# Score products of attention in a two-layer hybrid block: one fp32 matmul per map, or a sum of three fp32r products of split queries and keys

## The chip, the cores and the metric

The kernel runs on one core of a Trainium2 chip. The metric is the device time of one launch in microseconds (us), as the median of several launches. A core has a matrix engine (TensorE, in the profile PE, with its weight loads listed apart as PEld), a vector engine (VectorE, DVE), a scalar engine for activations and copies (ScalarE, ACT), a general engine (GpSimd, POOL) and a sync engine (SyncE, SP) that issues most DMAs. Each engine runs its own list of instructions in order, and they meet at semaphores. Matrix products land in PSUM, everything else lies in SBUF, both with 128 partitions.

## The reference

Two layers, each a half-step SwiGLU, a token mixing, and another half-step SwiGLU. Every one of these is wrapped in RMS norms and modulated by shift, scale and gate that come from a conditioning vector ("adaLN"). There are 256 latent tokens and 128 prompt tokens, 1024 channels wide. The mixing has one input projection whose columns feed four groups; two of them are attentions. The change is in their scores:

```python
s = jnp.einsum("bqhmd,bshmd->bhmqs", qb, k).astype(jnp.float32) * scale   # differential
p = jax.nn.softmax(s, axis=-1)
w = p[:, :, 0] - lam * p[:, :, 1]
...
s = jnp.einsum("bqkgd,bskd->bkgqs", qb, k).astype(jnp.float32) * scale    # grouped-query
p = jax.nn.softmax(s, axis=-1)
```

Differential attention has 4 heads with 2 maps each and keys of 32 channels; grouped-query attention has 4 query heads on 2 key heads of 64 channels. Latent queries see 128 cached context keys and the 256 latent keys, so 384; prompt queries see the 128 prompt keys. All inputs and outputs are fp32.

## The kernel before, in words

The 384 tokens are three tiles of 128 rows, t = 0 and 1 latent, t = 2 prompt. The stages follow each other: FFN, mixing, FFN, in each of two layers. The big products are written as sums of three products in a faster matmul type, fp32r: each fp32 operand is split into an upper half (its value cast to fp32r) and a lower half (what the cast left out), and the product is upper x upper + upper x lower + lower x upper (`mm3_b`, L541 to L544; `mm3_a`, L546 to L550; `rows_out`, L576 to L578). Weights come from memory in 128x1024 tiles `st` (DMA on SP's queue, L156), are cast by ScalarE (L167) and subtracted by VectorE (L168) into a tile `wu` that holds both halves. Tiles `ast` (L269) carry the adaLN weights, of which VectorE makes weighted sums during the FFNs (L279).

In the mixing stage (`mix`, L695; about 312 to 480 us in the first layer and 1070 to 1238 us in the second) the projection is computed in pieces, and while TensorE works on a later piece, the rows of an earlier one are normed, rotated and turned: `d_tail` (L844) transposes queries and keys of the grouped-query attention into PSUM, and ScalarE copies them to `qTg` and `kTg`; `qk_tail` does the same for the differential attention into `qTd` and `kTd` (L1005, L1007, L1008). The cached keys come already transposed, by two DMAs on POOL's queue straight into the first 128 columns of `kTd` and `kTg`. A convolution with 31 taps runs beside all this as a long row of VectorE instructions on `cacc` (L799).

`probs` (L868) makes one attention map: one plain fp32 matmul into a PSUM bank (L871), the negative row maximum by VectorE (L872), the exponential with its row sum by ScalarE (L876). The contraction is over 32 partitions (differential, two maps of a head on neighbouring groups of 32) or 64 (grouped-query). Then come three transposes of the map (L886), a copy (L888), and the products with the values (L894). A unit for each head, in three parts, is threaded between the pieces of projection. The order that results on each engine is set by a scheduler in the framework, which moves instructions within their dependencies, so the row of instructions isn't quite that of the code.

## Time and profile before

| | us |
|---|---|
| median of 3 runs | 1563.77 |
| lowest and highest of them | 1561.25, 1564.76 |
| the profiled execution | 1562.17 |
| its span, first to last instruction | 1560.4 |

TensorE's granted clock over the span is 0.986 of full speed. The profile lists each engine's instructions with start and duration. A plain fp32 matmul leaves two records, an fp32r one leaves one. A matmul's recorded duration holds its fill and drain, so successive matmuls overlap in the records, and what one takes of the engine's time is the distance from its start to the next start. In the timeline, rows of one kind that follow each other are joined, with their count behind an x; what stands in brackets is the idle time ahead of an instruction and what ended it.

### The profile page before, as it was taken

Reading aid. Unit: us, or ns where it says so; the run is one execution under the profiler, and the core shown is the slowest. Engines: PE = TensorE matmul, PEld = TensorE weight load, DVE = VectorE, ACT = ScalarE, POOL = GpSimd, SP = SyncE. Lnnn points to the kernel's source line nnn. Section 1 sums busy time; section 2 is a strip of 40 time slices with the busy share of each in tenths; the row PEclk is TensorE's granted clock in tenths of the full one; section 3 lists DMA queues with packets and bytes.
Section 4 is the critical chain, followed back from the end, with each engine's and each line's share of the span. In section 5 each row is a group of like instructions: output and inputs, shape, how many; then the busy total and the mean of one; then the engine's idle time right before and its main releaser. Section 6 shows DMA issues by size and latency. Waiting matters only on the chain. (4 is left out here: it accounts for less than half of the span.)

```text
span 1560.4 us, 20661 instructions
## 1 busy us (share of the span) xinstructions
PE 1500.0 (96%) x7924; PEld 1319.9 (85%) x7924; DVE 1050.7 (67%) x1454; ACT 633.7 (41%) x1103; POOL 126.4 (8%) x234
## 2 busy tenths in 40 slices
PE   6899999999999999999999999999999999999997
PEld 3699998776887899998879999887768879999885
DVE  3678879867887845677586766984788796333432
ACT  3442233263466632334263333434545764323331
POOL 1101000021001201000021000002100120000000
PEclk9999999998999999999999999999999999999998
DMA  8668767733224555675546656773322245444431
GB/s 307 227 222 261 236 211 236 245 109 98 68 70 145 150 177 179 212 233 172 189 150 215 206 188 200 231 234 110 112 73 92 72 160 175 134 132 138 135 122 41
DMA packets 73619, 260.13 MB, mean 167 GB/s; under 512 B 9728, under 2 KB 9856, under 8 KB 73520
## 3 DMA queue, kind: packets, MB, share of 16 engines
q1 hardware_dynamic: 68112, 246.32, 48.5%
q0 software_dynamic: 4976, 11.70, 2.7%
q8 instruction: 62, 1.02, 0.3%
q10 hardware_dynamic: 432, 0.79, 0.1%
q14 instruction: 37, 0.30, 0.1%
HBM read 256.36 MB, written 2.41 MB: 166 GB/s over the span
## 5 line engine op out<-in xcount | busy, mean ns | idle before, releaser
L168 DVE TENSOR_TENSOR wu<-st,wu 128x1024 fp32r<-128x1024 f32 x322 | 391.6, 1219 | 296.5 <-ACT wu L167 295.9
L167 ACT CAST wu<-st 128x1024 fp32r<-128x1024 f32 x322 | 337.0, 1050 | 585.4 <-DMA st<-ws 253.7
L549 PE MATMUL ps_f<-h,wu 128*128 128x384 f32 x1248 | 418.6, 335 | 0.0
L548 PE MATMUL ps_f<-h,wu 128*128 128x384 f32 x1248 | 418.4, 336 | 0.0
L550 PE MATMUL ps_f<-h,wu 128*128 128x384 f32 x1248 | 418.3, 335 | 0.0
L279 DVE SCALAR_TENSOR_TENSOR acc<-ast,sc,acc 128x1024 f32<-128x1024 f32 x224 | 281.6, 1281 | 27.5 <-DMA ast<-w_ada 26.9
L548 PEld LDWEIGHTS ps_f<-h,wu 128*128 128x128 f32 x1248 | 234.9, 188 | 7.8 <-issue 4.2
L550 PEld LDWEIGHTS ps_f<-h,wu 128*128 128x128 f32 x1248 | 235.0, 188 | 0.0
L549 PEld LDWEIGHTS ps_f<-h,wu 128*128 128x128 f32 x1248 | 235.0, 188 | 0.0
L576 PE MATMUL ps_o<-wu,hid_s 128*128 128x512 f32 x528 | 206.5, 391 | 0.0
L577 PE MATMUL ps_o<-wu,hid_s 128*128 128x512 f32 x528 | 206.0, 390 | 0.0
L578 PE MATMUL ps_o<-wu,hid_s 128*128 128x512 f32 x528 | 205.5, 389 | 0.0
L576 PEld LDWEIGHTS ps_o<-wu,hid_s 128*128 128x128 f32 x528 | 99.1, 188 | 26.1 <-issue 5.9
L578 PEld LDWEIGHTS ps_o<-wu,hid_s 128*128 128x128 f32 x528 | 99.1, 188 | 20.6
L577 PEld LDWEIGHTS ps_o<-wu,hid_s 128*128 128x128 f32 x528 | 99.1, 188 | 20.0
L543 PE MATMUL ps_j<-wu,h 128*128 128x512 f32 (+1 forms) x192 | 73.1, 381 | 5.3 <-DVE wu L168 5.3
L542 PE MATMUL ps_j<-wu,h 128*128 128x512 f32 (+1 forms) x192 | 74.5, 388 | 0.0
L544 PE MATMUL ps_j<-wu,h 128*128 128x512 f32 (+1 forms) x192 | 72.6, 378 | 0.0
L676 ACT ACTIVATE sg<-ps_f 128x384 f32<-128x384 f32 x78 | 38.0, 487 | 83.4 <-PE ps_f L550 79.3
L799 DVE SCALAR_TENSOR_TENSOR cacc<-upad,late,cacc 128x399 f32<-128x399 f32 x120 | 69.9, 630 | 0.0
L337 POOL DMA_DIRECT2D gd<-grow x24 | 11.7, 496 | 676.0 <-DVE grow L329 676.0
L677 DVE TENSOR_TENSOR hid<-sg,ps_f 128x384 f32<-128x384 f32 x78 | 42.9, 549 | 23.3 <-PE ps_f L550 23.3
(234 smaller groups left out, 1701.0 us busy)
## 6 DMA issues: line engine op xcount, KB each, us to landing
st<-ws SPq DMA_DIRECT2D x320, 512.0 KB, 3.9
ast<-w_ada SPq DMA_DIRECT2D x128, 512.0 KB, 4.4
a<-ada SPq DMA_DIRECT2D x16, 512.0 KB, 9.3
G<-gd POOLq DMA_DIRECT2D x12, 512.0 KB, 4.7
brow<-b_ada POOLq DMA_DIRECT2D x24, 64.0 KB, 5.6
prow<-norm_post POOLq DMA_DIRECT2D x24, 64.0 KB, 6.1
x<-x_sample SPq DMA_DIRECT2D x2, 512.0 KB, 5.2
x<-x_prompt SPq DMA_DIRECT2D x1, 512.0 KB, 8.9
```

What stands on the lines that cost most here:

```text
L167: nc.scalar.copy(out=u[:, 0, :], in_=x)
L168: nc.vector.tensor_tensor(out=u[:, 1, :], in0=x, in1=u[:, 0, :].bitcast(F32), op=ALU.subtract)
L279: nc.vector.scalar_tensor_tensor(out=self.acc[c], in0=w, scalar=s1, in1=self.acc[c], op0=ALU.mult, op1=ALU.add)
L542: nc.tensor.matmul(out, lhsT=hk(h, k, 0, tsl), rhs=wh, start=start, stop=False)
L543: nc.tensor.matmul(out, lhsT=hk(h, k, 0, tsl), rhs=wl, start=False, stop=False)
L544: nc.tensor.matmul(out, lhsT=hk(h, k, 1, tsl), rhs=wh, start=False, stop=stop)
L548: nc.tensor.matmul(out, lhsT=wh, rhs=hk(h, k, 0, sl), start=start, stop=False)
L549: nc.tensor.matmul(out, lhsT=wh, rhs=hk(h, k, 1, sl), start=False, stop=False)
L550: nc.tensor.matmul(out, lhsT=wl, rhs=hk(h, k, 0, sl), start=False, stop=stop)
L576: nc.tensor.matmul(out, lhsT=pr[:, 0, s, tsl], rhs=u[:, 0, hsl], start=(q == 0), stop=False)
L577: nc.tensor.matmul(out, lhsT=pr[:, 0, s, tsl], rhs=u[:, 1, hsl], start=False, stop=False)
L578: nc.tensor.matmul(out, lhsT=pr[:, 1, s, tsl], rhs=u[:, 0, hsl], start=False, stop=(q == n - 1))
```

## The change

The score of a map becomes three fp32r products over split queries and keys, accumulated in the same PSUM bank: upper x upper, upper x lower, lower x upper. Queries and keys therefore hold both halves, in tiles with one more dimension of 2. A new helper `halves` makes them: the upper one is ScalarE's copy, as before but in type fp32r, the lower one is a new VectorE instruction that reads the same source and subtracts the upper half. The two maps of a differential head are now issued together, product by product in turn; the scheduler moves these too. The cached keys come by one DMA into a buffer `kc` and are split from there.

The larger tiles need room in SBUF. The pool of the `ast` tiles moves from the whole kernel into each FFN's scope; the scratch `sink` of the squares is half as wide; the wide copy of the conditioning vector goes to the setup's pool; `grow` has one buffer instead of two; the buffers of type `c3` are three instead of four, with one of their own for `upad` and `zT`.

```diff
-    ap_ = ctx.enter_context(tc.tile_pool(name="adap", bufs=2))
...
-        with tc.tile_pool(name=nm("fp"), bufs=1) as fp:
+        with tc.tile_pool(name=nm("fp"), bufs=1) as fp, tc.tile_pool(name=nm("adap"), bufs=2) as ap_:
...
-            kTd = mp.tile([P, 2, TOK], F32, name=nm("kTd"))
+            kTd = mp.tile([P, 2, 2, TOK], F32R, name=nm("kTd"))
...
-            nc.gpsimd.dma_start(out=kTd[:, :, 0:P], in_=a["cache_kT"][l, :, 0:2])
-            nc.gpsimd.dma_start(out=kTg[:, 0:P], in_=a["cache_kT"][l, :, 2])
+            kc = mp.tile([P, TOK], F32, tag="p", name=nm("kc"), bufs=4)
+            nc.gpsimd.dma_start(out=kc.rearrange("p (c n) -> p c n", c=3), in_=a["cache_kT"][l])
+
+            def halves(hi, lo, src, scale=1.0):
+                nc.scalar.mul(hi, src, scale)
+                nc.vector.scalar_tensor_tensor(
+                    out=lo, in0=src, scalar=scale, in1=hi.bitcast(F32), op0=ALU.mult, op1=ALU.subtract
+                )
...
+            halves(kTd[:, 0, :, 0:P], kTd[:, 1, :, 0:P], kc[:, 0:256].rearrange("p (c n) -> p c n", c=2))
+            halves(kTg[:, 0, 0:P], kTg[:, 1, 0:P], kc[:, 256:384])
...
-                nc.scalar.mul(
-                    qTg[:, :, t * P : (t + 1) * P], pt[:, 0:256].rearrange("p (g n) -> p g n", g=2), 64 ** -0.5
-                )
-                nc.scalar.copy(out=kTg[:, (t + 1) * P : (t + 2) * P] if t < 2 else kTgp, in_=pt[:, 256:384])
+                tsl, ksl = slice(t * P, (t + 1) * P), slice((t + 1) * P, (t + 2) * P)
+                halves(
+                    qTg[:, 0, :, tsl], qTg[:, 1, :, tsl], pt[:, 0:256].rearrange("p (g n) -> p g n", g=2),
+                    64 ** -0.5,
+                )
+                k0, k1 = (kTg[:, s, ksl] if t < 2 else kTgp[:, s, :] for s in range(2))
+                halves(k0, k1, pt[:, 256:384])
...
-            def probs(t, st, idx, lhsT, rhs):
+            def probs(t, st, maps):
+
                 nk = TOK if t < 2 else P
-                ps = bank(nm("ps_s"))
-                nc.tensor.matmul(ps[:, 0:nk], lhsT=lhsT, rhs=rhs, start=True, stop=True)
...
+                pss = [bank(nm("ps_s")) for _ in maps]
+                for a_, b_ in ((0, 0), (0, 1), (1, 0)):
+                    for ps, (idx, lhsT, rhs) in zip(pss, maps):
+                        nc.tensor.matmul(
+                            ps[:, 0:nk], lhsT=lhsT(a_), rhs=rhs(b_), start=(a_ + b_ == 0), stop=(a_ == 1)
+                        )
...
-                        r = 32 * (2 * (hd % 2) + m)
-                        pm.append(probs(t, st, i0 + m, qTd[r : r + 32, c, tsl], kt[r : r + 32, c, :]))
+                    rows = [slice(32 * (2 * (hd % 2) + m), 32 * (2 * (hd % 2) + m) + 32) for m in range(2)]
+                    pm = probs(
+                        t, st,
+                        [
+                            (i0 + m, lambda s, r=r: qTd[r, s, c, tsl], lambda s, r=r: kt[r, s, c, :])
+                            for m, r in enumerate(rows)
+                        ],
+                    )
...
-                nc.scalar.mul(qTd[:, :, t * P : (t + 1) * P], pq[:, 0:2, :], 32 ** -0.5)
-                nc.scalar.copy(out=kTd[:, :, (t + 1) * P : (t + 2) * P] if t < 2 else kTdp, in_=pq[:, 2:4, :])
+                tsl, ksl = slice(t * P, (t + 1) * P), slice((t + 1) * P, (t + 2) * P)
+                halves(qTd[:, 0, :, tsl], qTd[:, 1, :, tsl], pq[:, 0:2, :], 32 ** -0.5)
+                k0, k1 = (kTd[:, s, :, ksl] if t < 2 else kTdp[:, s] for s in range(2))
+                halves(k0, k1, pq[:, 2:4, :])
```

The order on the engines changes as follows. In its rows the names are those of the code with running numbers (`ps_j` a projection's PSUM bank, `ps_s` a map's, `wu` a split weight tile, `h` the normed input).

TensorE at the first two latent maps of the grouped-query attention in the first layer, before:

```order
L544 MATMUL ps_j325_3117<-wu76_2952,h235_2555 128x512
L871 MATMUL ps_s328_3137<-kTg282_2809,qTg284_2811 128x384
L542 MATMUL ps_j325_3117<-wu76_2952,h235_2555 128x512
L543 MATMUL ps_j325_3117<-wu76_2952,h235_2555 128x512
L544 MATMUL ps_j325_3117<-wu76_2952,h235_2555 128x512
L542 MATMUL ps_j325_3117<-wu77_3112,h236_2556 128x512
L543 MATMUL ps_j325_3117<-wu77_3112,h236_2556 128x512
L544 MATMUL ps_j325_3117<-wu77_3112,h236_2556 128x512
L542 MATMUL ps_j325_3117<-wu77_3112,h236_2556 128x512
L543 MATMUL ps_j325_3117<-wu77_3112,h236_2556 128x512
L544 MATMUL ps_j325_3117<-wu77_3112,h236_2556 128x512
L871 MATMUL ps_s332_3169<-kTg282_2809,qTg284_2811 128x384
```

and after the change:

```order
L545 MATMUL ps_j327_3126<-wu77_3121,h237_2558 128x512
L887 MATMUL ps_s330_3148<-kTg283_2812,qTg285_2814 128x384
L543 MATMUL ps_j327_3126<-wu77_3121,h237_2558 128x512
L544 MATMUL ps_j327_3126<-wu77_3121,h237_2558 128x512
L545 MATMUL ps_j327_3126<-wu77_3121,h237_2558 128x512
L887 MATMUL ps_s334_3182<-kTg283_2812,qTg285_2814 128x384
L887 MATMUL ps_s330_3148<-kTg283_2812,qTg285_2814 128x384 x2
L887 MATMUL ps_s334_3182<-kTg283_2812,qTg285_2814 128x384 x2
```

The two maps stood nine projection products apart. Now the first product of the first map stands alone, and its other two follow, with all three of the second map, after three projection products.

TensorE at the seventh pair of differential maps of the first layer (`ps_pT` are transposes of earlier maps, `ps_pv` products with values), before:

```order
L886 MATMUL ps_pT456_3841<-early_87,p435_3749 128x128 x3
L894 MATMUL ps_pv424_3700<-Vd285_2812,wt449_3804 128x64 x3
L871 MATMUL ps_s463_3862<-kTd279_2806,qTd281_2808 128x384
L871 MATMUL ps_s465_3867<-kTd279_2806,qTd281_2808 128x384
L548 MATMUL ps_j455_3828<-h235_2555,wu83_3495 128x384
```

and after:

```order
L551 MATMUL ps_j457_3895<-h235_2556,wu82_3482 128x384
L887 MATMUL ps_s465_3929<-kTd280_2809,qTd282_2811 128x384
L907 MATMUL ps_pT450_3863<-early_84,p429_3768 128x128 x3
L887 MATMUL ps_s466_3930<-kTd280_2809,qTd282_2811 128x384
L887 MATMUL ps_s465_3929<-kTd280_2809,qTd282_2811 128x384
L887 MATMUL ps_s466_3930<-kTd280_2809,qTd282_2811 128x384
L887 MATMUL ps_s465_3929<-kTd280_2809,qTd282_2811 128x384
L907 MATMUL ps_pT458_3908<-early_84,p438_3814 128x128 x3
L915 MATMUL ps_pv426_3755<-Vd286_2815,wt451_3867 128x64 x3
L887 MATMUL ps_s466_3930<-kTd280_2809,qTd282_2811 128x384
```

The pair's two matmuls stood side by side; its six products now stand in three places, with transposes between them, and in the middle one they alternate between the two banks.

VectorE ahead of the weight split that ends TensorE's wait at 378 us (rows 7 below), in the first layer (`dr` are rotated rows, `cacc` the convolution, `ss` is the sum of squares from which POOL makes the root `rstd`, `dn` the normed rows, `rt` a rotated part, `st` the row maxima), before:

```order
L726 TENSOR_TENSOR dr314_3049<-dn313_3044,late_89 128x384
L799 SCALAR_TENSOR_TENSOR cacc298_2936<-upad289_2820,late_89,cacc298_2936 128x399
L731 TENSOR_TENSOR dr314_3049<-dr314_3049,rt315_3050 128x384
L799 SCALAR_TENSOR_TENSOR cacc298_2936<-upad289_2820,late_89,cacc298_2936 128x399 x2
L814 TENSOR_REDUCE ss6319_3094<-sqd318_3090 128x6
L799 SCALAR_TENSOR_TENSOR cacc298_2936<-upad289_2820,late_89,cacc298_2936 128x399
L820 TENSOR_TENSOR dn322_3100<-ps_j316_3059,rstd321_3098 128x2x2x64
L826 TENSOR_TENSOR dn322_3100<-ps_j316_3059,rstd321_3098 128x128
L831 TENSOR_TENSOR dn322_3100<-dn322_3100,gqk_126 128x256
L831 TENSOR_TENSOR dn322_3100<-dn322_3100,gqk_126 128x128
L168 TENSOR_TENSOR wu77_3112<-st77_2950,wu77_3112 128x1024
L168 TENSOR_TENSOR wu78_3160<-st78_2955,wu78_3160 128x1024
```

and after:

```order
L733 TENSOR_TENSOR dr316_3056<-dn315_3051,late_86 128x384
L715 SCALAR_TENSOR_TENSOR qTg285_2814<-ps_dT319_3079,qTg285_2814 128x2x128
L738 TENSOR_TENSOR dr316_3056<-dr316_3056,rt317_3057 128x384
L715 SCALAR_TENSOR_TENSOR kTg283_2812<-ps_dT319_3079,kTg283_2812 128x128
L806 SCALAR_TENSOR_TENSOR cacc300_2939<-upad291_2823,late_86,cacc300_2939 128x399 x2
L824 TENSOR_REDUCE ss6321_3103<-sqd320_3099 128x6
L806 SCALAR_TENSOR_TENSOR cacc300_2939<-upad291_2823,late_86,cacc300_2939 128x399
L830 TENSOR_TENSOR dn324_3109<-ps_j318_3066,rstd323_3107 128x2x2x64
L836 TENSOR_TENSOR dn324_3109<-ps_j318_3066,rstd323_3107 128x128
L841 TENSOR_TENSOR dn324_3109<-dn324_3109,gqk_125 128x256
L841 TENSOR_TENSOR dn324_3109<-dn324_3109,gqk_125 128x128
L168 TENSOR_TENSOR wu77_3121<-st77_2957,wu77_3121 128x1024
```

Between the rotation of the tile before (`dr`) and the sum of squares, two lower halves (L715) now stand, and two convolution instructions (`cacc`) where there were three; the third stands further up, ahead of the first tile's sum of squares. The next rows are another lower half between the first weight split and the second, and one behind the second, ahead of the first row maximum.

## Rows read from the trace of the kernel before

**Rows 1.** From the page: busy time of each engine, its share of the span and its instructions; and the shares by engine of the chain of work that ended last.

```profile
PE 1500.0 (96%) x7924; PEld 1319.9 (85%) x7924; DVE 1050.7 (67%) x1454; ACT 633.7 (41%) x1103; POOL 126.4 (8%) x234
...
PE 41%; DVE 2%; POOL 1%; issue 1%; ACT 1%; DMA 1%; DVEq 0%; POOLq 0%; ACTq 0%
```

**Rows 2.** Busy time of the engines in the two mixing stages: the stretch and its length, busy us of PE, PEld, DVE, ACT and POOL (with instructions), TensorE's granted clock, DMA share, GB/s.

```profile
312.00:480.00 168.00, 159.35 (x826) 128.06 (x827) 126.74 (x270) 92.32 (x223) 22.92 (x43) 0.96 0.26 83
1070.00:1238.00 168.00, 159.63 (x843) 128.16 (x841) 127.54 (x274) 94.99 (x229) 23.35 (x43) 0.98 0.26 85
```

**Rows 3.** Groups of the score line on TensorE: tiles, shape, count of records, busy us in total and mean ns of one, idle time before.

```profile
L871 PE MATMUL ps_s<-kTd,qTd 32*128 32x384 f32 x64 | 19.4, 533 | 0.0
...
L871 PE MATMUL ps_s<-kTg,qTg 64*128 64x384 f32 x32 | 16.0, 583 | 0.0
...
L871 PE MATMUL ps_s<-kTdp,qTd 32*128 32x128 f32 x32 | 3.9, 321 | 0.0
...
L871 PE MATMUL ps_s<-kTgp,qTg 64*128 64x128 f32 x16 | 3.9, 322 | 0.0
```

**Rows 4.** TensorE's timeline at a lone latent map of the grouped-query attention, and at a lone prompt map: start, duration, line, operation.

```profile
373.09 0.39 PE L543 MATMUL ps_j<-wu,h 128*128 128x512 f32 x1
373.32 0.40 PE L544 MATMUL ps_j<-wu,h 128*128 128x512 f32 x1
373.65 0.91 PE L871 MATMUL ps_s<-kTg,qTg 64*128 64x384 f32 x2
374.49 0.50 PE L542 MATMUL ps_j<-wu,h 128*128 128x512 f32 x1
374.82 0.40 PE L543 MATMUL ps_j<-wu,h 128*128 128x512 f32 x1
...
412.31 0.48 PE L871 MATMUL ps_s<-kTgp,qTg 64*128 64x128 f32 x2
412.73 0.44 PE L903 MATMUL ps_mo<-early,mo 128*128 128x128 f32 x2
```

**Rows 5.** TensorE's timeline at three pairs of differential maps, two of latent and one of prompt queries, each with the instruction behind it.

```profile
435.88 0.91 PE L871 MATMUL ps_s<-kTd,qTd 32*128 32x384 f32 x4
436.73 0.45 PE L549 MATMUL ps_j<-h,wu 128*128 128x384 f32 x1
...
440.18 1.23 PE L871 MATMUL ps_s<-kTd,qTd 32*128 32x384 f32 x4
441.34 0.45 PE L548 MATMUL ps_j<-h,wu 128*128 128x384 f32 x1
...
463.93 0.49 PE L871 MATMUL ps_s<-kTdp,qTd 32*128 32x128 f32 x4
464.35 0.44 PE L548 MATMUL ps_j<-h,wu 128*128 128x384 f32 x1
```

**Rows 6.** TensorE's timeline in the projections: neighbouring fp32r products over all 128 rows, on 256 and on 384 columns.

```profile
408.64 0.29 PE L544 MATMUL ps_j<-wu,h 128*128 128x256 f32 x1
408.76 0.28 PE L542 MATMUL ps_j<-wu,h 128*128 128x256 f32 x1
...
433.13 0.34 PE L550 MATMUL ps_j<-h,wu 128*128 128x384 f32 x1
433.31 0.34 PE L548 MATMUL ps_j<-h,wu 128*128 128x384 f32 x1
```

**Rows 7.** The stall of the first layer's mixing: TensorE's instruction that ended it, VectorE's timeline ahead of it, and VectorE's busy time in three stretches behind it (stretch, length, busy us, TensorE's granted clock, DMA share, GB/s).

```profile
378.30 0.80 PE L543 MATMUL ps_j<-wu,h 128*128 128x512 f32 x1 [2.62 <-DVE wu L168]
...
375.96 0.42 DVE L820 TENSOR_TENSOR dn<-ps_j,rstd 128x256 f32<-128x256 f32 x1 [1.51 <-POOL rstd L460]
376.30 0.28 DVE L826 TENSOR_TENSOR dn<-ps_j,rstd 128x128 f32<-128x128 f32 x1
376.50 0.62 DVE L831 TENSOR_TENSOR dn<-dn,gqk 128x256 f32<-128x256 f32 x2
377.03 2.36 DVE L168 TENSOR_TENSOR wu<-st,wu 128x1024 fp32r<-128x1024 f32 x2
...
380.00:390.00 10.00, 8.21 (x16) 0.60 0.43 143
390.00:400.00 10.00, 8.99 (x18) 1.00 0.16 52
400.00:410.00 10.00, 9.15 (x18) 1.00 0.04 14
```

**Rows 8.** Groups of VectorE instructions with a PSUM source on 128x256 and 128x128.

```profile
L465 DVE TENSOR_TENSOR mTd<-ps_mo,mTd 128x256 fp32r<-128x256 f32 x6 | 2.5, 413 | 1.9 <-ACT mTd L464 1.9
...
L826 DVE TENSOR_TENSOR dn<-ps_j,rstd 128x128 f32<-128x128 f32 x6 | 1.7, 280 | 0.0
```

**Rows 9.** ScalarE's timeline at the second square of the norm ahead of the mixing (first tile), and TensorE's first product of the mixing.

```profile
318.15 0.60 ACT L527 ACTIVATE sink<-ps_o 128x512 bf16<-128x512 f32 x1 [2.04 <-PE ps_o L578]
...
331.20 0.39 PE L542 MATMUL ps_j<-wu,h 128*128 128x512 f32 x1
```

**Rows 10.** The first FFN: TensorE's stall, and SP's issues of `ast` and `st` tiles.

```profile
75.65 1.09 PE L642 MATMUL ps_ht<-early,sg 128*128 128x128 f32 x4 [4.61 <-DVE sg L639]
...
45.16 0.90 SPq L269 DMA_DIRECT2D ast<-w_ada  x2
...
60.58 1.42 SPq L156 DMA_DIRECT2D st<-ws  x2
```

67 lines of the change are left out of this document (36 added, 31 removed).

## The prediction

> **What bounds the kernel now.** I read the page first. TensorE is busy for 96% of the span and VectorE for 67%, and the chain that ended last is TensorE's wherever it is put down to an engine by more than a few per cent [rows 1]. Then I cut out the two mixing stages, the only places where the change touches instructions that compute. In each the reader is to see TensorE busy for about 159 of 168 us, VectorE for 127 [rows 2]. So a score that takes less or more time on TensorE moves the end by that much, and VectorE's additions cost only what makes TensorE wait. Third, the groups of the score line: 64 and 32 records on 384 columns, 32 and 16 on 128, thus 144 records for 72 maps, two for each [rows 3]. Their mean durations overlap each other, so I price them by starts in the timeline, not by these means.
>
> **What a score costs before.** A lone 384-column map runs from 373.65 to the next start at 374.49, 0.84 us; a lone 128-column one from 412.31 to 412.73, 0.42 [rows 4]. 256 more columns thus cost 0.42 us in two records, 0.21 each; a 384-column record streams for 0.315 and has 0.105 beside that, a 128-column one streams for 0.105 and has 0.105 beside it. I read this fixed 0.105 as a load of weights that stands open. Full-height fp32r products, three to a product sum just as the change builds them, show no such part: 384 columns step by 0.18 us, 256 by 0.12 [rows 6], close to half a record's streaming. Going into a block of scores costs 0.33 instead of 0.23 for the matmul before it, and the one behind it takes 0.33 too [rows 4]: about 0.2 per block.
>
> **What the change makes of it.** Each map becomes three fp32r products with contraction over 32 or 64 rows. The trace has no such product, so its price is bounded: below by the full-height step (0.18 for 384 columns, half of 0.12 for 128), above by a record of today (0.42 and 0.21). I take half the record's streaming and keep the open load: 0.16 + 0.105 = 0.265 and 0.053 + 0.105 = 0.158, as the nearest rows in height are today's scores. Three make 0.79 and 0.47, against 0.84 and 0.42.
>
> The Trainium skill, "TensorE: Matmul & The Clock Gate", section "The mechanism" in its part on packing small matmuls, says that a weight load overlaps running matmuls only where its row group is another one. By that rule three products of one map, which share a row group, each leave their load open, which is the value that I take. The full-height products of [rows 6] share all row groups and yet step without it, so there the trace does not agree, and the rule may fail for the small ones too. With it the sum is the one below, without it that of rival A.
>
> Per layer, then:
> - Grouped-query maps: eight of 384 columns, 8 x -0.05 = -0.4; four of 128, +0.2. In the new order two prompt heads stand in one block, which saves one block's 0.2. Sum -0.4.
> - Differential pairs on 384 columns, eight. Before, two maps on other row groups run together: four records in 0.85, elsewhere 1.16 [rows 5]. By where each pair stands, two lie apart at 0.84 a map, four take 0.85 and two some 1.15: 3.36 + 3.40 + 2.30 = 9.06. After, it is the order that decides: where products alternate between the maps, a pair costs 0.79; where three of one stand ahead of three of the other, TensorE takes them in order and the second map begins beside the third product of the first, 5 x 0.265 = 1.32. From the new order (two maps apart; two, two, one, one; three and three, twice; cut in two; alternating; cut in three; alternating): 1.58 + 1.06 + 1.32 + 1.32 + 1.06 + 0.79 + 1.46 + 0.79 = 9.38 (1.46 is 4 x 0.265 and two blocks more). Sum +0.3.
> - Differential pairs on 128 columns, four: 0.42 before [rows 5], 0.47 after, one of them cut into two blocks: 4 x 0.05 + 0.2 = +0.4.
>
> TensorE: +0.3 per layer, +0.7 in both (unrounded).
>
> **VectorE.** It makes the lower halves: 14 instructions per layer, of 128x256 or 128x128 like those of [rows 8] (413 and 280 ns), which step by 0.34 and 0.20 [rows 7], about 4.2 us per layer. ScalarE already writes the upper halves in place of the copies that it made; only the cached keys' two are new. The cached keys' halves fall between the two squares of the post-norm, where ScalarE waits 2.04 us for TensorE [rows 9]: nothing. Were they late they would delay the norm, and TensorE starts the stage's first product only at 331.20 [rows 9]. The other lower halves stand between 372 and 425 us. There TensorE stands still once for VectorE, 2.62 us until 378.30 for a weight split [rows 7]; in the new order the row up to that split holds two lower halves more and no convolution instruction less (one has only moved further up in it). Where VectorE idles there, it waits for the root that POOL makes from its own sum of squares (1.51 us [rows 7]), so that idle time covers nothing: the split ends by 0.34 + 0.20 later, +0.54 per layer, +1.1 in both. Behind it, from 380 to 410, VectorE is busy for 8.21 + 8.99 + 9.15 of 30 us [rows 7]; that leaves about 3.6 us for some 3.0 us of lower halves. I take them as hidden, with C below if not.
>
> **The moved pool.** The adaLN tiles now live in each FFN's scope. In the first FFN their first two loads, which were issued at 45.16 [rows 10], wait for ScalarE to end its last modulation of the setup, whose room they take; two weight tiles go ahead of them, two behind. SP's queue is in order, so the weights behind wait too, but those were issued only at 60.58 before [rows 10], when a buffer came free. The bytes are the same. A stall of 4.61 us stands at 75.65 [rows 10], fed by late weights; I take zero, between -4.6 (it goes) and +3 (two more tiles of 512 KB share the time before it). The smaller sink and the single grow buffer change nothing that TensorE waits for; the cached keys' single load is off the path by the same slack as their halves.
>
> **The sum.** +0.7 + 1.1 = +1.8. The profiled execution took 1562.17 us (span 1560.4 and 1.8 around it), so 1564.0 for its like. The median of the three runs lies 1.6 higher, at 1563.77; on its level the forecast is 1565.6. Below 0.2%, 3.1 us, a measurement of this kernel can't be told from no change: 1560.6 to 1566.9.
>
> **Rivals.**
> *A, loads hide inside a block.* Only the first product of a block leaves its load open. For it: full-height products hide theirs, and each lone map of today is itself the first of its block. Against it: the pair at 440.18 takes 1.16 though it lies in one block. Then 384 columns cost 0.585 (-0.25), 128 columns 0.265 (-0.155): grouped-query -2.0 - 0.6 - 0.2 = -2.8, pairs -2.0 by the same order, prompt pairs -0.4; -5.2 per layer, -10.4 in both, with the stall's +1.1 about -9: 1554.5.
>
> *B, 128 columns stay dear.* No fp32r product on fewer than 256 columns stands in the trace. If one streams there as slowly as a whole fp32 map does (0.21) and has one load open, it costs 0.32 instead of 0.158. There are 12 steps for the grouped-query and 12 for the pairs, per layer: 48 x 0.16 = +7.7, and with the forecast's +1.8 +9.5: 1573.3. It is slower from a step of about 0.19 on. Place: the prompt blocks near 412 and 464 us. For it: three times as many instructions on the shortest rows; against: 256 columns already scale with their width [rows 6].
>
> *C, VectorE sets the pace.* The lower halves come late behind the weight splits and convolutions between 380 and 410 us; TensorE waits for the second and third product or for the exponentials. If their 3.0 us find no gap in either layer: +6.0, with the +1.8 1571.6. From the point at which the 3.6 us of room are gone it decides. Against: TensorE's clock is at half speed there (0.60 [rows 7]), and a later start only moves that stretch.
>
> The Trainium skill, "TensorEngine Tiling (Array Packing)", "Key Properties", has a change of tiling mode drain TensorE. The 0.2 per block above agrees with it; by it an order that cuts a pair into more blocks costs, and A would lose a little of its gain.
>
> **How the numbers follow.** Forecast 0.42, A 0.34, B 0.15, C 0.09. The forecast's own range is 1562 to 1570: within 0.2% 0.60, slower 0.33, faster 0.07. A is faster in 0.93, no change in 0.07. B is slower in 0.92, C in 0.88, otherwise no change. Faster: 0.03 + 0.31 = 0.34; no change: 0.25 + 0.02 + 0.01 + 0.01 = 0.30, rounded up; slower 0.36. The range for 8 in 10 goes from 1553, leaving out the lower third of A, to 1573, leaving out the upper half of B and some of C.
>
> **What would show it.** The distance from a lone 384-column block's first start to the next instruction: 0.79 for the forecast, 0.6 for A, while a 128-column block shows 0.47, 0.27 or, for B, 0.95. Pairs with three ahead of three: 1.3 against 1.0. VectorE's step: TensorE's wait for the split at 378 grows by about 0.5; for C new waits of TensorE for lower halves or exponentials, over 1 us each, before 410. The first FFN: the wait at 75.65 moves by less than 3 us. Wrong would be above all a step of the small fp32r products far from 0.265 and 0.158, or a changed time outside the mixing stages.

## The result: 1584.61 us, 1.3% slower, and the profile after

The changed kernel takes 1584.61 us in the median of four runs (1581.32 to 1585.39), the kernel before 1564.26 beside it: a ratio of 1.0127 [1.0109, 1.0145]. That is 20 us more; 1.8 were forecast, and the range ended at 1573. The profiled execution took 1581.32 us, its span is 1579.5.

The page after, against [rows 1]: 72 more matmul records on TensorE, 29 more instructions on VectorE, and a span longer by 19 us.

```profile
PE 1507.9 (95%) x7996; PEld 1333.8 (84%) x7996; DVE 1058.4 (67%) x1483; ACT 640.3 (41%) x1107; POOL 129.5 (8%) x232
...
PE 17%; issue 1%; POOL 0%; ACT 0%; DVE 0%; POOLq 0%; DVEq 0%; ACTq 0%
```

The mixing stages in the columns of [rows 2], with shorter stretches of the first one:

```profile
312.00:480.00 168.00, 154.85 (x837) 128.12 (x836) 129.88 (x278) 93.69 (x221) 23.14 (x37) 0.95 0.25 82
1070.00:1238.00 168.00, 156.64 (x841) 128.32 (x839) 126.66 (x266) 88.72 (x208) 22.88 (x41) 0.96 0.27 87
380.00:390.00 10.00, 10.00 (x42) 7.76 (x43) 7.69 (x15) 4.22 (x10) 0.00 (x0) 0.78 0.17 54
390.00:400.00 10.00, 10.00 (x54) 7.92 (x52) 9.86 (x20) 4.85 (x10) 0.00 (x0) 1.00 0.17 54
400.00:410.00 10.00, 8.13 (x55) 6.90 (x56) 7.29 (x16) 3.35 (x9) 0.54 (x1) 1.00 0.04 15
...
440.00:460.00 20.00, 20.00 (x123) 17.17 (x123) 15.68 (x43) 12.11 (x29) 2.59 (x4) 0.94 0.16 54
460.00:480.00 20.00, 17.37 (x112) 15.41 (x111) 15.19 (x43) 16.62 (x36) 4.08 (x6) 0.92 0.31 102
```

TensorE is busy 4.5 and 3.0 us less than before in the same stretches, and the clock dips more often: in the first layer three times where it did twice, the last two at 440 to 480 us, and in the second three times where it did once. By the granted clock of the trace the two mixings, cut as below, spend 17.1 us each at the lower of the two clock levels, 1.2 GHz, where they spent 13.7 and 6.8. TensorE does not have more work: it waits more, and what it does runs more of its time at that level. The score groups, against [rows 3], went from 19.4 to 17.7, 16.0 to 14.8, 3.9 to 4.8 and 3.9 to 4.0:

```profile
L887 PE MATMUL ps_s<-kTd,qTd 32*128 32x384 f32 x96 | 17.7, 376 | 0.0
L887 PE MATMUL ps_s<-kTg,qTg 64*128 64x384 f32 x48 | 14.8, 420 | 0.0
...
L887 PE MATMUL ps_s<-kTdp,qTd 32*128 32x128 f32 x48 | 4.8, 292 | 0.0
L887 PE MATMUL ps_s<-kTgp,qTg 64*128 64x128 f32 x24 | 4.0, 284 | 0.0
```

TensorE's timeline after, in pieces: the waits of the first mixing, a lone map of 384 and of 128 columns, a latent pair with three products ahead of three and a prompt pair whose products alternate (with what stands behind each), and the head of the FFN behind the mixing.

```profile
374.54 0.80 PE L544 MATMUL ps_j<-wu,h 128*128 128x512 f32 x1 [3.87 <-DVE wu L168]
...
385.55 0.79 PE L887 MATMUL ps_s<-kTg,qTg 64*128 64x384 f32 x3
386.27 0.50 PE L543 MATMUL ps_j<-wu,h 128*128 128x512 f32 x1
...
404.14 0.55 PE L907 MATMUL ps_pT<-early,p 128*128 128x128 f32 x3 [1.25 <-ACT p L896]
405.31 0.88 PE L915 MATMUL ps_pv<-Vg,wt 128*128 128x64 f32 x6 [0.62 <-ACT wt L909]
...
416.59 0.55 PE L887 MATMUL ps_s<-kTgp,qTg 64*128 64x128 f32 x3
417.07 0.39 PE L543 MATMUL ps_j<-wu,h 128*128 128x256 f32 x1
...
433.08 0.80 PE L887 MATMUL ps_s<-kTd,qTd 32*128 32x384 f32 x6
433.81 0.44 PE L550 MATMUL ps_j<-h,wu 128*128 128x384 f32 x1
...
461.49 0.55 PE L887 MATMUL ps_s<-kTdp,qTd 32*128 32x128 f32 x6
461.97 0.44 PE L549 MATMUL ps_j<-h,wu 128*128 128x384 f32 x1
...
476.45 0.36 PE L907 MATMUL ps_pT<-early,p 128*128 128x128 f32 x1 [1.91 <-DVE p L987]
...
531.30 1.09 PE L502 MATMUL ps_t<-early,xn 128*128 128x128 f32 x8 [0.64 <-DVE xn L492]
534.28 0.52 PE L543 MATMUL ps_gu<-wu,h 128*128 128x512 f32 x1 [1.65 <-ACT h L465]
```

The stall of [rows 7] has grown from 2.62 to 3.87 us; the waits at 404 to 405 for the exponential and the copy of a map, and that of 1.91 before the last pair's transposes, are new or longer (before the last one was 0.79).

VectorE's row ahead of that stall, with the stage's first product after the change (before, it stands at 331.20). First the norm of the first tile before; then the first product, the same norm and the weight split after:

```profile
361.85 0.42 DVE L820 TENSOR_TENSOR dn<-ps_j,rstd 128x256 f32<-128x256 f32 x1 [1.52 <-POOL rstd L460]
```

```profile
326.44 0.39 PE L543 MATMUL ps_j<-wu,h 128*128 128x512 f32 x1
...
358.09 0.42 DVE L830 TENSOR_TENSOR dn<-ps_j,rstd 128x256 f32<-128x256 f32 x1 [1.53 <-POOL rstd L461]
...
373.27 1.22 DVE L168 TENSOR_TENSOR wu<-st,wu 128x1024 fp32r<-128x1024 f32 x1
```

From that norm to the split VectorE takes 15.18 us in both kernels: the two lower halves stand where one convolution instruction was, which now stands ahead of that norm. But the row starts later, 31.65 us behind the stage's first product where it was 30.65, and the split ends TensorE's wait 1.00 us later; TensorE came to it 0.25 us earlier. In the second layer the split is 0.67 us later and TensorE 0.57 earlier.

**Where the 19 us of span came from.** I cut both traces at TensorE's first product of each stage and subtracted. A mixing goes from its first projection product to the first product of the FFN behind it. A head is the gate and up projection's first stretch, from there to the first transpose of the gated rows; there is one in the FFN behind each mixing and one in the second layer's first FFN.

| stretch | before | after | difference |
|---|---|---|---|
| first FFN, from its first product | 310.2 | 305.3 | -4.9 |
| mixing, layers 1 and 2 | 185.2 + 182.8 | 191.7 + 192.1 | +15.9 |
| the three heads | 20.2 + 20.1 + 20.2 | 23.8 + 21.4 + 23.8 | +8.5 |
| all else | | | -0.4 |

Inside the mixings I added up each kind of slot (start to next start, less the wait ahead of it). Waits grew by 5.6 and 5.3 us, the slots of the projection products into and out of the stage, 576 in each layer of both kernels, by 2.0 and 4.8, and scores fell by 1.1 in each (19.84 to 18.75); the rest is +0.1 and +0.4. The products' growth goes with the time at the lower level, some 3 and 10 us more of it.

### The profile page after: what moved, and what is told of

Read it like the earlier page. It is cut to its first block, busy times and chain, and to the rows that moved or that the text cites. A ratio compares the mean times of both kernels' runs of the same rounds, so it can differ in the third digit from the quotient of the medians.

```text
span 1579.5 us, 20882 instructions
## 1 busy us (share of the span) xinstructions
PE 1507.9 (95%) x7996; PEld 1333.8 (84%) x7996; DVE 1058.4 (67%) x1483; ACT 640.3 (41%) x1107; POOL 129.5 (8%) x232
## 5 line engine op out<-in xcount | busy, mean ns | idle before, releaser
L578 PEld LDWEIGHTS ps_o<-wu,hid_s 128*128 128x128 f32 x528 | 99.1, 188 | 20.1
```

The lines of the kernel that those rows point to most:

```text
L578: nc.tensor.matmul(out, lhsT=pr[:, 0, s, tsl], rhs=u[:, 1, hsl], start=False, stop=False)
```

## The experiments

Fourteen kernels. The last columns come from their profiled runs by the cuts above: mixing of layer 1, of layer 2, and the three heads together.

| run | us | ratio [95%] | mixing 1 | mixing 2 | heads |
|---|---|---|---|---|---|
| before | 1564.26 | 1 | 185.2 | 182.8 | 60.5 |
| after | 1584.61 | 1.0127 [1.0109, 1.0145] | 191.7 | 192.1 | 69.0 |
| sink_only | 1577.03 | 1.0091 [1.0065, 1.0117] | 186.2 | 186.2 | 66.4 |
| pools_only | 1574.62 | 1.0079 [1.0055, 1.0103] | 187.5 | 187.9 | 64.2 |
| after_xn | 1581.11 | 1.0125 [1.0102, 1.0149] | 192.5 | 193.8 | 61.0 |
| after_order | 1580.51 | 1.0129 [1.0103, 1.0154] | 188.6 | 191.2 | 67.9 |
| wide_scratch | 1577.64 | 1.0100 [1.0077, 1.0122] | 194.0 | 191.3 | 59.8 |
| wide_and_order | 1575.18 | 1.0085 [1.0060, 1.0110] | 191.1 | 191.3 | 60.9 |
| products_alone | 1575.72 | 1.0090 [1.0065, 1.0116] | 189.1 | 186.3 | 68.5 |
| halves_alone | 1579.21 | 1.0117 [1.0089, 1.0146] | 191.5 | 187.2 | 63.4 |
| gqa_split_only | 1582.30 | 1.0115 [1.0084, 1.0147] | 192.9 | 192.5 | 60.4 |
| diff_split_only | 1569.50 | 1.0042 [1.0019, 1.0066] | 188.0 | 187.3 | 60.9 |
| fewer_conv_ahead | 1566.61 | 1.0031 [1.0011, 1.0050] | 185.4 | 185.9 | 60.9 |
| plain_fewer_ahead | 1560.38 | 0.9987 [0.9970, 1.0004] | 181.4 | 179.7 | 60.5 |
| split_fewer_ahead | 1578.74 | 1.0102 [1.0075, 1.0129] | 188.8 | 188.0 | 67.9 |
| split_two_ahead | 1565.07 | 1.0021 [1.0005, 1.0038] | 185.0 | 182.8 | 60.9 |

The median of before was 1561.60 to 1562.23 beside the experiments, so ratios are compared, not medians. The last columns are one execution each. The mean granted clock of before's runs beside the experiments goes from 0.984 to 0.993, and its profiled run had 0.986; 0.004 of 1560 us is 6 us, an estimate of what chance can do to such a run as a whole.

**1. The scratch of the squares.** `sink_only` is the kernel before with one edit, `pools_only` has all the edits on tiles and pools and none on the scores (`kTd` and `kTg` are filled by their own DMAs, as before):

```diff
-    sink = cp.tile([P, D], BF16, name="sink")
+    sink = cp.tile([P, 512], BF16, name="sink")
...
-                out=sink[:, hsl], in_=x[t][:, hsl], func=AF.Square, scale=D ** -0.5,
+                out=sink, in_=x[t][:, hsl], func=AF.Square, scale=D ** -0.5,
```

> The kernel before, with the scratch of the squares half as wide and nothing else. Theory scratch: the two squares of a norm now write the same scratch, so the scheduler sets a weight cast of ScalarE between them, the norm comes later and TensorE's transposes stand later in its row; the heads of the FFNs behind the mixing lose what they lose in the changed kernel, 3.6 + 1.3 + 3.6 us, and each mixing some 0.8 at its norms: 8 to 11 us slower than before. Theory scores (the loss comes from the scores and their lower halves alone): within 2 us of before.

> The kernel before, with all the memory edits (pool of the ast tiles in the FFN's scope, narrow scratch, one grow buffer, three c3 buffers, wide conditioning copy in the setup's pool) and the plain fp32 scores. Theory scratch: the loss of the scratch, 8 to 11, less the 5.2 us that the changed kernel gains in the first FFN, which I put to the moved pool: 3 to 6 us slower than before. Theory scores: 5 us faster than before, since only the gain of the first FFN is left.

Without any split product these cost 14 and 12 us by their ratios, more than the theory of the scratch had (8 to 11, 3 to 6) and against that of the scores. The heads grow by 5.9 and 3.7 us, the mixings by 1.0 and 3.4, 2.3 and 5.1. So by the ratios 12 of the 20 us of the change are there before a score is split. The late start of VectorE's row is there too: the first tile's norm stands 31.77 us (`sink_only`) and 31.91 us (`pools_only`) behind the first product of the first layer's mixing (30.65 before), 31.71 and 31.66 in the second layer (31.17 before). ScalarE's timeline shows how the heads lose, ahead of the FFN behind the first mixing; before:

```profile
514.64 0.64 ACT L486 ACTIVATE sink<-x 128x512 bf16<-128x512 f32 x1
515.17 0.20 ACT L486 ACTIVATION_READ_ACCUMULATOR sink<-x 128x1 f32 x1
515.26 0.62 ACT L486 ACTIVATE sink<-x 128x512 bf16<-128x512 f32 x1
```

after:

```profile
516.66 0.64 ACT L487 ACTIVATE sink<-x 128x512 bf16<-128x512 f32 x1
517.19 0.20 ACT L487 ACTIVATION_READ_ACCUMULATOR sink<-x 128x1 f32 x1
517.28 1.05 ACT L167 CAST wu<-st 128x1024 fp32r<-128x1024 f32 x1
518.23 0.64 ACT L487 ACTIVATE sink<-x 128x512 bf16<-128x512 f32 x1
```

Both squares of a norm now write the same bytes, which nobody reads. Between them the scheduler places a weight cast of 1.05 us, the norm's sum is ready later, and TensorE's transposes stand further back in its row: six projection products ahead of them before, twelve after. The head waits 1.65 us for `h` at 534.28 and then runs at 0.85 of the clock from 535 to 545, where before it had 1.00.

The rest of `pools_only`'s expectation, that moving the pool of the `ast` tiles shortens the first FFN, is not borne out: `pools_only` and the changed kernel have the same rows there on TensorE and SyncE, and on VectorE up to the lower halves of the cached keys at its end, and the stretch takes 312.7 and 305.3 us. It takes 305.3 to 312.7 in the thirteen kernels with the moved pool and 310.2 to 314.4 in the three without, so the -4.9 in the table above can't be put down to an edit.

`after_xn` and `wide_scratch` take the shared bytes away from the changed kernel, one by writing the norm's squares into a tile that is overwritten anyway, the other by 8-bit scratch of full width, with the same number of bytes:

```diff
-                out=sink, in_=x[t][:, hsl], func=AF.Square, scale=D ** -0.5,
+                out=xn[:, hsl], in_=x[t][:, hsl], func=AF.Square, scale=D ** -0.5,
```

```diff
-    sink = cp.tile([P, 512], BF16, name="sink")
+    sink = cp.tile([P, D], mybir.dt.uint8, name="sink")
...
-                out=sink, in_=x[t][:, hsl], func=AF.Square, scale=D ** -0.5,
+                out=sink[:, hsl], in_=x[t][:, hsl], func=AF.Square, scale=D ** -0.5,
```

> The changed kernel, with the squares of the norm ahead of each stage written into that norm's own output tile, half by half, in place of the shared scratch. Theory scratch: the heads come back, 8 to 10 us faster than the changed kernel, some 1575. Theory scores: within 2 us of the changed kernel.

> The changed kernel, with the scratch of the squares at its full width again, in 8-bit integers so that it takes the same bytes (nothing reads it). Theory scratch: heads as before, 20.2 us each, so 8.5 us less; mixing as in the changed kernel: 1574 to 1577. If the scratch also shapes the mixing, up to 3 us less again. Theory scores: within 2 us of the changed kernel (1584.6).

Both bring the heads back to 61.0 and 59.8 us. ScalarE in `wide_scratch`, in the same place, has its two squares side by side again:

```profile
520.42 0.64 ACT L487 ACTIVATE sink<-x 128x512 uint8<-128x512 f32 x1
520.96 0.20 ACT L487 ACTIVATION_READ_ACCUMULATOR sink<-x 128x1 f32 x1
521.05 0.63 ACT L487 ACTIVATE sink<-x 128x512 uint8<-128x512 f32 x1
```

The heads' 8.5 us are thus shown to come from the scratch, though how much it costs there goes with the rest of the row (5.9 in `sink_only`, 2.9 in `halves_alone` below). In all, the 8 us that both expectations had don't come back: `after_xn` gains 0.0002 by the ratios and `wide_scratch` 0.0027, some 4 us with an interval about as large. In `after_xn`'s profile the mixings grow by 0.8 and 1.6 and the first FFN took longer. In `wide_scratch` the first tile's norm is back at 30.77 us, and yet its mixings are as long as the changed kernel's; the mixing's 16 us have another cause beside the scratch.

**2. Who reads the transposed rows first.** ScalarE and VectorE take the upper and the lower halves from one PSUM tile. ScalarE's timeline after:

```profile
363.82 0.38 ACT L714 ACTIVATE qTg<-ps_dT 128x256 fp32r<-128x256 f32 x1
367.95 0.28 ACT L714 ACTIVATE kTg<-ps_dT 128x128 fp32r<-128x128 f32 x1 [3.76 <-DVE qTg L715]
...
374.86 0.28 ACT L714 ACTIVATE kTg<-ps_dT 128x128 fp32r<-128x128 f32 x1 [5.38 <-DVE qTg L715]
```

The keys' upper half needs nothing of VectorE, and yet it starts only once VectorE has made the queries' lower half: in this program the two engines read one PSUM tile in turn. The Trainium skill, "PSUM — Partial Sum Buffer", "PSUM bank collisions raise a hardware error", says that ScalarE and VectorE must not read one bank on the same partitions at the same time and that software has to order them; the trace agrees as far as the order goes, with waits of 3.76 and 5.38 us. `after_order` puts both upper halves down first:

```diff
-                nc.vector.scalar_tensor_tensor(
+                return lambda: nc.vector.scalar_tensor_tensor(
...
-                halves(
+                q1 = halves(
...
-                halves(k0, k1, pt[:, 256:384])
+                run([halves(k0, k1, pt[:, 256:384]), q1])
```

> The changed kernel, with the upper halves of query and key both issued ahead of their lower halves. Theory turn-taking: the key's upper half waits on ScalarE for the query's lower half on VectorE, as both read one PSUM tile, and holds up ScalarE's row (idle 3.76, 5.38 and more) and then VectorE's and TensorE's; without that wait 3 to 8 us faster than the changed kernel. Theory load (VectorE's 14 instructions more are the cost, in any order): within 2 us of it. Theory scratch says nothing of it.

`wide_and_order` has this and the wide scratch:

```diff
+    sink = cp.tile([P, D], mybir.dt.uint8, name="sink")
...
+                run([halves(k0, k1, pt[:, 256:384]), q1])
```

> The same, and both upper halves issued ahead of the lower ones. Theory turn-taking: 2 to 4 us faster than wide_scratch, 1571 to 1574. Theory load: the same as wide_scratch.

ScalarE's wait is gone, but the intervals with and without the edit overlap widely in both comparisons, as the theory of load has it. TensorE's stall only changes its name in `after_order`, 3.74 us for the lower half of the keys itself, and stays at the weight split in `wide_and_order` (3.66 and 3.98). Behind the turn stands the next wait for VectorE, which ends at nearly the same time; the turn alone is not what cost the time here.

**3. Products or halves.** `products_alone` multiplies upper by upper three times and makes no lower halves; `halves_alone` makes them, and has one plain fp32 matmul over the upper halves per map:

```diff
-                nc.vector.scalar_tensor_tensor(
-                    out=lo, in0=src, scalar=scale, in1=hi.bitcast(F32), op0=ALU.mult, op1=ALU.subtract
-                )
...
-                            ps[:, 0:nk], lhsT=lhsT(a_), rhs=rhs(b_), start=(a_ + b_ == 0), stop=(a_ == 1)
+                            ps[:, 0:nk], lhsT=lhsT(0), rhs=rhs(0), start=(a_ + b_ == 0), stop=(a_ == 1)
```

```diff
-                for a_, b_ in ((0, 0), (0, 1), (1, 0)):
-                    for ps, (idx, lhsT, rhs) in zip(pss, maps):
...
+                for ps, (idx, lhsT, rhs) in zip(pss, maps):
+                    nc.tensor.matmul(
+                        ps[:, 0:nk], lhsT=lhsT(0).bitcast(F32), rhs=rhs(0).bitcast(F32), start=True, stop=True
+                    )
```

> The changed kernel without the 14 lower halves of each layer: all three products of a map use the upper halves, so the lower parts are left out of the sums. Theory load (VectorE's lower halves and what they displace cost the mixing): mixing near pools_only, 146.6 us in each layer, 4 us per layer below the changed kernel, so about 1576. Theory products (three products and their order cost it): mixing stays at 150 to 151, 1583 or more.

> The changed kernel with the lower halves made, but each map is one plain fp32 matmul on the upper halves, so the lower parts are left out of the sums. Theory load: mixing stays at 150 to 152 us in each layer; 1583 or more, since the products' gain of 1.1 us per layer goes too. Theory products: mixing back near 146.6, about 1576.

The stalls divide cleanly. The one near 378 us is 3.87 in `halves_alone`, as in the changed kernel, and gone in `products_alone`, where 2.30 us stand further on at another instruction. That is `pools_only`'s picture: there too the weight split comes ahead of the third tile's norm, nothing waits for it, and 2.90 us stand further on, so the lower halves bring back a stall that the memory edits alone had moved. The one at the end of the stage is 2.46 us in `products_alone` and 0.80, as before, in `halves_alone`. Both kernels hold the memory edits. Above `pools_only` (1.0079) the products cost 0.0011 and the halves 0.0038, together 0.0049, and 0.0048 lie between `pools_only` and the changed kernel; with intervals of 0.0025 to each side this does not say which part is the larger. The profiles speak against a plain sum. The expectations count a mixing up to its first output product: that takes 146.7 and 146.5 us in `pools_only`, 146.2 and 145.7 in `products_alone`, 147.8 and 146.0 in `halves_alone`, and 150.8 and 151.0 with both. `products_alone` is where the theory of load put it, `halves_alone` is where the rival put it in the mixing, and between the two by its time: up to there the loss comes mostly with both together. Nor do the memory edits and the split add: the memory edits cost 0.0079 without the split (the scratch alone 0.0091), the split 0.0100 with the wide scratch, and both 0.0127. Each edit gives the scheduler another row, and I can't say of the mixing's 16 us how much is load and how much order.

**4. Which attention.** With the wide scratch, one attention split and the other left in fp32 (`gqa_split_only`, then `diff_split_only`):

```diff
-            kTd = mp.tile([P, 2, 2, TOK], F32R, name=nm("kTd"))
+            kTd = mp.tile([P, 1, 2, TOK], F32, name=nm("kTd"))
...
+                        ((0, 0),),
```

```diff
-            kTg = mp.tile([P, 2, TOK], F32R, name=nm("kTg"))
+            kTg = mp.tile([P, 1, TOK], F32, name=nm("kTg"))
...
+                        t, box["st"], [(hd, lambda s: qTg[vs, s, g, tsl], lambda s: kt[vs, s, :])], ((0, 0),)
```

> wide_scratch with the split scores in the grouped-query attention alone; the differential one is plain fp32 on unsplit tiles, as before. Theory order (the loss in the mixing is in waits that the new order of the engines makes, three per layer): the stall near 47 us of the stage (4.0 us in two parts, 2.6 before) and that at 78 (1.9) stay, that at its end (1.9 and 0.7) goes; both mixing stages 4 to 6 us longer than before, clock included: 1570 to 1574. Theory work (lower halves and products cost by their number): half of the 12 products and 14 lower halves of each unit are left, so half of wide_scratch's loss in the same places, the end among them: about 1570, with a wait left at the end.

> wide_scratch with the split scores in the differential attention alone. Theory order: the stall near 47 is 2.6 as before, none at 78, the waits at the end (1.9 and 0.7) stay: each mixing stage 2 to 4 us longer than before, 1566 to 1570. Theory work: half of wide_scratch's loss, about 1570, spread over the stage.

In both kernels the unsplit attention still has its cached keys copied from `kc`, and the two maps of a differential head issued together. Splitting the grouped-query scores alone costs as much as splitting both (1.0115 against 1.0100; neither theory had it above 1574 us); splitting the differential ones costs 0.0042, which fits both theories. The waits of TensorE (us in total, times, longest), first with the grouped-query split:

```profile
PE ps_dT L857 <- DVE dn L841: 5.2, 2, 2.6
...
PE ps_j L544 <- DVE wu L168: 2.8, 2, 1.4
PE ps_pT L907 <- ACT p L896: 2.5, 2, 1.2
```

and with the differential one:

```profile
PE ps_j L544 <- DVE wu L168: 5.2, 2, 2.6
PE ps_pT L903 <- DVE p L983: 3.8, 2, 1.9
```

Two stalls of 2.6 and 1.4 us, close together at the place of [rows 7], in each layer and the wait for the exponential come with the grouped-query split; the wait of 1.9 at the end comes with the pairs, while the stall of [rows 7] stays as before. That points to the grouped-query lower halves, which stand on VectorE just where TensorE already waited for it. It is not shown that they alone are the cost: `halves_alone` has them and no wait of a microsecond for the exponential.

**5. Relieving VectorE there.** `fewer_conv_ahead` is `wide_and_order` with three convolution instructions after each block of rows where four were; `split_two_ahead` has two:

```diff
-CONVD = 4
+CONVD = 3
```

```diff
-CONVD = 4
+CONVD = 2
```

> wide_and_order with three in place of four convolution instructions of VectorE threaded behind each grouped-query projection (CONVD 3), so that the two lower halves of a tile take the place of one. If VectorE's row up to the weight split sets the stall near 47 us (3.7 to 4.0), it falls by about 0.5 per tile, to 2.5 to 3, and the low clock behind it with it: 2 to 5 us faster than wide_and_order (1575). If the place in the order decides and not the length of the row, the stall stays above 3.5 and the time within 2 us.

> The changed kernel with the wide 8-bit scratch, both upper halves put down first, and two taps after each block. Theory 'VectorE's row up to the first lower halves sets the stall': with three taps 3.60 us of stall are left on the lower half of the second prompt block, and one tap of 0.55 us less per block takes 0.5 to 1.6 us off it in each layer; 1561 to 1566. Rival 'the taps come back later': each tap not placed ahead stands in the mixing's later stretch, where VectorE is busy 9 tenths at 390 to 420, and delays the softmax there: 1567 to 1573.

With three, the ratio falls from 1.0085 to 1.0031. The stall in its place, and the mixings, `wide_and_order` first and then `fewer_conv_ahead`:

```profile
377.33 0.44 PE L890 MATMUL ps_s<-kTg,qTg 64*128 64x384 f32 x1 [3.60 <-DVE kTg L715]
```

```profile
312.00:480.00 168.00, 156.37 (x851) 128.98 (x847) 128.63 (x276) 90.72 (x218) 24.73 (x43) 0.96 0.26 86
1070.00:1238.00 168.00, 157.16 (x832) 128.49 (x830) 125.53 (x264) 85.79 (x204) 21.82 (x39) 0.95 0.26 87
```

```profile
312.00:480.00 168.00, 156.70 (x870) 130.47 (x869) 132.35 (x289) 95.47 (x228) 24.93 (x43) 0.98 0.26 88
1070.00:1238.00 168.00, 156.17 (x865) 130.13 (x864) 131.79 (x288) 95.02 (x228) 24.09 (x42) 0.98 0.26 88
```

TensorE waits about as long as in `wide_and_order` (13.1 and 13.3 us against 13.7 and 13.6), but the granted clock is 0.98 in place of 0.96 and 0.95: each mixing spends 6.8 us at the lower level in place of 17.1, and the slots of its projection products sum to 3.9 and 3.1 us less. Neither theory foresaw that: the stall stays above 3.5, the sign of the second, and the time falls by more than the first had. Which wait the clock follows is open; the sum of the waits it is not. With two the waits fall too, to 11.2 and 9.2; the ratio, 1.0021, overlaps with that of three.

Is that the split's load undone, or a gain that the kernel before would have too? `plain_fewer_ahead` is the kernel before, `split_fewer_ahead` the changed kernel, each with that one edit:

```diff
-CONVD = 4
+CONVD = 3
```

```diff
-CONVD = 4
+CONVD = 3
```

> The kernel before, with one edit: three convolution taps are put on VectorE after each block of latent rows where four were (CONVD 3); the scores stay plain fp32. Theory 'VectorE's row at the stall was made too long by the split, and only by it': the kernel before has 2.62 us of stall at 378 and half-clock extra of 6.7 and 3.9 us per layer; taking the taps out shortens its stall to about 1.4 to 2.0 and gains 0 to 3 us, 1561 to 1564, so most of the 9 us that the same edit gave with the split is the split's own load undone. Rival 'the taps are a cost of their own': it gains as much here as with the split, 6 to 10 us, 1554 to 1558, and then the split is worth about -10 us whatever the taps.

> The changed kernel as it is (narrow shared scratch, lower halves put on the row in its order), with three taps after each block where four were. Theory 'three separate costs that add': the taps give back 7 to 10 us as they did with the wide scratch and the other order, the heads behind the norms keep their 23.8 us (2 x 3.6 over before), so 1572 to 1577. Rival 'the taps and the order of the halves only work together': 1579 to 1584, no gain worth naming.

By the ratios the kernel before gains 2 us, at most 5 by its interval, against 8 with the split (1.0085 to 1.0031). The profiled mixings say less clearly that this is load undone: they fall by 3.7 and 3.1 us with plain scores, where the time at the lower level falls from 13.7 and 6.8 us to 6.8 and 3.4 and the waits don't fall at all (9.5 and 9.4), and by 5.7 and 5.4 with the split. So a part of the 8 us belongs to the split; that it is most of them isn't shown. On the changed kernel as it is the edit gives 4 us, between the two theories, and the intervals overlap: with the weight split out of the way, TensorE now stands 4.00 us for the upper half of the keys, and that is late by its turn. TensorE, and under it ScalarE:

```profile
379.31 0.69 PE L887 MATMUL ps_s<-kTg,qTg 64*128 64x384 f32 x1 [4.00 <-ACT kTg L714]
```

```profile
378.98 0.28 ACT L714 ACTIVATE kTg<-ps_dT 128x128 fp32r<-128x128 f32 x1 [4.88 <-DVE qTg L715]
```

That looks as if the two causes cover each other: taking away the turn alone (experiment 2) gives 0 to 2 us, the load alone 4, both together 11 (`wide_scratch` to `fewer_conv_ahead`). With an interval of some 4 us on each ratio, and the load alone tried only with the narrow scratch, that is not shown. At three instructions the split still costs 4.0 and 6.2 us of mixing over the plain scores (185.4 and 185.9 against 181.4 and 179.7).

`plain_fewer_ahead` and `fewer_conv_ahead` also show what the products save, since both have little time at the lower clock (3.4 and 6.8 us in layer 2): all scores of that layer take 17.94 us of TensorE plain and 18.03 split. One block of the split ones stands at the lower clock (1.23 for 0.72), so at equal clock the saving is about 0.4 us. Of the 19.84 before, only 0.7 were the clock, one map of 1.57 where the others take 0.84:

```profile
380.74 1.64 PE L871 MATMUL ps_s<-kTg,qTg 64*128 64x384 f32 x2
```

The other 1.2 us or so are order: before, two pairs stand as lone maps, 0.84 each, where a pair side by side takes 0.84 in all; in `plain_fewer_ahead` only one does.

No version with split scores beats the kernel before. `plain_fewer_ahead` can't be told from it.

## Why the prediction was wrong

- **"The smaller sink and the single grow buffer change nothing that TensorE waits for."** Wrong, and shown so: the sum had the memory edits at nothing, and without any split they cost 12 us (`pools_only`; the scratch alone 14). In the changed kernel 8.5 us of it are in the heads. I looked at sizes, not at which writes now meet in the same bytes and so must keep an order.
- **VectorE's step.** The place was right, the size was not: the stall grew by 1.25 us per layer, not 0.54. From the first tile's norm to the split the row is no longer than before, 15.18 us; it starts 1.00 us later in the first layer, which the kernels with the narrow scratch and no split show too, and TensorE comes 0.25 us earlier. So 0.54 was not too small a price for the halves; what else moves the row was missing. The turn-taking at the PSUM tile was not in the sum at all; in `split_fewer_ahead` it makes a stall of 4.00.
- **"I take them as hidden."** The 3.0 us of lower halves fit into VectorE's idle time, but idle time summed over 30 us is no slack. They did not stay hidden: with the wide scratch, where the heads are as before, the split still costs 0.0100, some 16 us. Rival C's sign showed, over 1 us for an exponential before 410 us (404.14). C's 6 us were still too few, since it looked at 380 to 410 alone; the wait of 1.91 at the end of the stage (0.79 before) lay beyond it. How much of the 16 us is VectorE's load and how much the order of the rows stays open.
- **The clock.** The sum had no term for it. The mixings wait 14.1 and 14.5 us in place of 8.5 and 9.2 and spend 17.1 us each at the lower level in place of 13.7 and 6.8. That the waits bring the dips is argued, not shown: `fewer_conv_ahead` waits 13.1 and 13.3 and spends only 6.8. I argued against C that "a later start only moves that stretch"; but there are more dips, at 440 to 480 us.
- **The products.** Lone maps came out near their price, 0.72 measured on 384 columns (forecast 0.79) and 0.48 on 128 (forecast 0.47), but by luck: a load that stands open in each product is not what the trace shows. The steps at 385.55 are 0.28, 0.18 and 0.26; the middle one is the full-height step of [rows 6], so inside a block the load is hidden, as A had it, and each edge of the block costs about 0.1, the far one of which A had not. On 128 columns the inner steps of a block of six are 0.11 (near 411 us), where B had 0.32 and A 0.05. The whole maps refute B (0.95) and A on the small ones (0.27), and A's 0.585 for the large ones is twice as far off as the forecast. The pairs I mis-sized: three ahead of three takes 0.73 at 433.08 and 1.05 at 437.24, not 1.32, since the second map's products run beside the first's on other rows of the array even in that order. Prompt pairs take 0.48 where they stand in one block. TensorE gained 1.1 us per layer where I had a loss of 0.3, and the clock took from that gain: 0.7 us of the scores before are the lower level, about 1 us of those after, an estimate from the two maps at 375.70 and 377.89 (2.52 us where others take 0.72 each).
- **The moved pool** at nothing: not contradicted; any effect is smaller than the scatter of the stretch.

The forecast's sum was thus wrong by what waits for whom, and by a clock that it left out, hardly by what an instruction costs.

## What to carry to other kernels

Where VectorE already makes TensorE wait, an instruction put ahead of that place can cost its length, and may cost clock behind it; look for the order on its row, not for its idle share, and try moving work that is not yet due (here convolution instructions) out of the way first. A write-only scratch that is shared by neighbouring instructions is still an order between them, and narrowing it can cost about as much as the edit it makes room for (here 0.0091 and 0.0100 alone). Measure the edits that make room by themselves. And before trading one fp32 matmul for three fp32r ones at small contraction, compare the slots at the same clock and in the same order: here 0.84 against 0.72 on 384 columns, 0.42 against 0.48 on 128, in sum 0.4 to about 1.4 us a layer, an estimate from the sums above, by how the pairs stand.

## What the runs showed of the hardware that I had not expected

- Six products of two maps on different row groups take 0.73 us (433.08), about as long as three of one map alone (0.72), although three of one stand ahead of three of the other. The next pair in that order takes 1.05: there the second map starts 0.32 us after the first, right after ScalarE has ended an exponential (437.51), for which it seems to wait.

```profile
437.24 1.12 PE L887 MATMUL ps_s<-kTd,qTd 32*128 32x384 f32 x6
```

- Three products of one map, which share their row group, take 0.72 us on 384 columns: 0.28 for the first, 0.18 for the second and 0.26 for the third, which starts at 386.01. By the Trainium skill, "TensorE: Matmul & The Clock Gate", "The mechanism", each would leave its whole weight load open. The trace does not agree inside a block, where the step is that of a full-height product.

```profile
386.01 0.33 PE L887 MATMUL ps_s<-kTg,qTg 64*128 64x384 f32 x1
```

- ScalarE's square into 8-bit scratch takes 0.63 to 0.64 us, as into 16-bit.
- The first FFN took 305.3 and 312.7 us in two profiled runs with the same rows on TensorE and SyncE; a single profile can't price an edit there below that. Most of the difference is one wait of TensorE for `ps_mod`, 1.66 us at 160.6 and 7.91 at 165.0.
